# First block's mixer: HGRN gate and queries by plain float32 products, doublings among the values' products, transposes behind gate tiles

## The chip, the cores and the metric

The kernel runs on one core of one Trainium2 chip, as one launch. Its time is device microseconds (us) of that core, and a kernel's time is the median of its runs. The engines are TensorE (PE, with its weight loads as PEld), VectorE (DVE), ScalarE (ACT), GpSimd (POOL) and SyncE (SP), which issues most transfers. Each works through its own list of instructions in order; an instruction waits for those of other engines by semaphores.

## The reference, cut to what matters

The program is a two-block transformer on 256 tokens of width 1024 in float32. The change lies in the first layer's mixer alone, which is an HGRN2 half and an RWKV7 half, side by side, under one input and one output projection:

```python
u = h @ w_in                       # h [256,1024]; HGRN q, f, i, g of 512 columns each, then RWKV
hq, hf, hi, hg, ur = split(u)
f = lb + (1 - lb) * sigmoid(hf)
o_a = hgrn2_chunked(silu(hq), 1 - f, hi, log(f))      # scores decayed by cumulated log f
o_a = rms_norm(o_a) * silu(hg)
...                                                   # r, k, v, decay, a, kk, g out of ur
y = rwkv7_scan(r, decay, k, v, kk, a)                 # per head: state*w + sa*b + v*k
o_b = (head_layer_norm(y) + bonus) * g
return concat(o_a, o_b) @ w_out
```

Behind it come the first layer's feed-forward part, an attention layer and the second block with its experts. None of that is touched.

## The kernel before

**Stages.** The mixer takes about the first 186 us of the span. `proj` (its slabs of 256 columns of `w_in` are 1 MB each) makes a projection: SP loads a slab, ACT rounds half of it (128x1024) to float32r (`L116`, a cast), DVE takes the rest, what the rounding lost (`L117`), and PE adds three products for each of eight k-tiles and each tile of 128 features: high weights by high input (`L137`), low weights by high input (`L138`), high weights by low input (`L139`), all 128x256. A projection of 512 columns is four such tiles. The input `h` is split the same way once, in `hT`. `dense_tok` does the values (512 columns in two slabs, 48 products of 512 columns), with tokens on the partitions.

**Order.** RWKV's projections come first. Then come the HGRN gate `f` (`hE`, columns 512 to 1023), the queries (columns 0 to 511), the values `hv`, the decayed scores in nine levels (`l`, 0 to 8, `L828` and `L861`), the outputs `oo`, the output gate (columns 1536 to 2047, "gate tiles") and `w_out`. Beside these runs RWKV's chunked form in pieces: `pairs` (the pairwise products `L638`, whose results DVE evicts in `L631`, `L642` and `L645`, then `L650`, `L658`, `L659`), an inverse of 32x32 triangular blocks on DVE (`L582` and `L584`, 31 steps of two dependent instructions each), `levels` (the "doublings", which put inverses of 32 together to 64 and 128: `L678`, `L692`, `L702`) and `chain` (states and outputs, ending in transposes of `yy`, `L782`). These are generators: `tick(n)` lets the next one emit up to n pieces at the point of the program where it is called. A scheduler then orders each engine's list by its own estimates and by what is pinned: `keep_in_program_order` pins an instruction to its place in the program, `issue_after` puts one behind another.

**Buffers.** `psa` gives one of four `acc` buffers of PSUM, `psb` one of the `pb` buffers. Two of the `acc` hold `X` (products `L650`, copied by ACT in `L652`) until that copy. A slab's buffer is free for the next slab when its last reader is done: before, that is DVE's `L117`. SP's list is in order: a slab that waits for its buffer holds back what stands behind it, and so does the inverse's way to memory and back (`L587` out, `L593` in), which waits for the last step of the inverse.

Of the kernel before, what the change touches and what calls it, by code (L numbers as in the profile page):

```python
# [19 lines left out]
S = 256  # L20
# [32 lines left out]
def tile_body(ctx, tc, a, out, stop=None, dbg=None):  # L53
# [281 lines left out]
    def mixer0():  # L335
# [16 lines left out]
        def t2(shape, name):  # L352
            return RW.tile(shape, F32, name=name, tag="t2", bufs=5)
# [28 lines left out]
        spin(6)  # L382
        hT = pair("xT")
        for k in range(KT):
            t = t2([128, S], "hf0")
            V.scalar_tensor_tensor(t, raw[k // 2][:, k % 2 * 256:k % 2 * 256 + 256], col("attn_norm0", k), rsB, op0=mult, op1=mult)
            A.copy(hT[0][:, k, :], t)
            if k % 2:
                pooled = G.tensor_tensor(hT[1][:, k, :], t, hT[0][:, k, :], sub)  # L389
            else:  # L390
                done = V.tensor_tensor(hT[1][:, k, :], t, hT[0][:, k, :], sub)
# [22 lines left out]

        def proj(c0, use, eng=(None, None), steps=0):

            t = slab(a["w_in_ar"][:, c0:c0 + 256], KT, 256, 2 if c0 == 3584 else 1)
            for i in range(2):
                with tc.issue_after(done.ins) if c0 == 3584 and i else nullcontext():
                    w = split_tile(t[:, :, i * 128:(i + 1) * 128], KT, 128, eng[i])  # L420
                p = psa()[:, 0:256]
                mm_feat3(p, w, hT, KT)
                use(i, p)
                tick(steps)
# [196 lines left out]
        def pairs():  # L621
# [32 lines left out]
            for j2 in range(2):  # L654
# [12 lines left out]
                yield  # L667

        def levels():


            def first(l, b):
                o = 8 * b
                Wm = t2([128, 8, l], "Wm")
                p = psb()[:, 0:8 * l]
                for i in range(8):
                    for r in ((0, 64) if l == 32 else (64,)):
                        T.matmul(p[(r if l == 32 else 0):(r + 64 if l == 32 else 64), i * l:i * l + l],  # L678
                                 El[r:r + 64, o + i, (r if l == 32 else 0):(r + 64 if l == 32 else 64)],
                                 Tu[r:r + 64, o + i, (r + 32 if l == 32 else 64):r + 64], start=True, stop=True)  # L680
                n = 128 if l == 32 else 64
                A.copy(Wm[0:n], p[0:n].rearrange("p (h c) -> p h c", h=8))
                return l, b, Wm
# [38 lines left out]
        def chain():  # L722
# [55 lines left out]
            for b in range(2):  # L778
                bs = slice(b * 128, b * 128 + 128)
                p = psb()  # L780
                for j in range(4):
                    T.transpose(p[:, j * 128:(j + 1) * 128], ys[b][:, j * 128:(j + 1) * 128], ident)  # L782
                z = t2([128, 4, 128], "z")
# [9 lines left out]
        for j2 in range(2):  # L793
            proj(512 + 256 * j2, lambda i, p: V.tensor_scalar(hE[:, 2 * j2 + i, :], p, -80.0, None, op0=amax), steps=3)
        A.activation(hE, hE, AF.Exp, scale=-1.0)
# [10 lines left out]
        for j2 in range(2):  # L806
            def useq(i, p):
                th = RW.tile([128, S], F32, name="th")
                A.activation(th, p, AF.Tanh, scale=0.5)
                V.scalar_tensor_tensor(q[:, 2 * j2 + i, :], th, 1.0, p, op0=add, op1=mult)  # L810
            proj(256 * j2, useq, steps=2)
        hv = h4([128, 2, 512], "hv")
# [9 lines left out]
        for l in range(9):  # L822
# [33 lines left out]
            if m < 128:  # L856
                for b in range(2):
                    bs = slice(b * 128, b * 128 + 128)
                    p = psa()
                    for h in range(4):  # L860
                        T.matmul(p[:, h * 128:(h + 1) * 128], z[:, h, bs], z[:, h, bs], start=True, stop=True)  # L861
                    V.copy_predicated(part(ST[:, b], l - 1, 1), half4(lvl[:, l - 1, :], l - 1, 1, 4),
                                      part(p.rearrange("p (h c) -> p h c", h=4), l - 1, 1))
                tick()
            else:
# [3 lines left out]
                A.copy(STx, p.rearrange("p (h c) -> p h c", h=4))  # L869
        tick(2)  # L870

# [16 lines left out]
        for j2 in range(2):  # L888
            def useg(i, p):
# [4 lines left out]
                A.activation(hg[:, j, :], th, AF.Copy, scale=hon[:, j:j + 1])  # L894
            proj(1536 + 256 * j2, useg, steps=(2,2)[j2])

        for b in range(2):
            bs = slice(b * 128, b * 128 + 128)
            p = psa()
            for j in range(4):  # L900
# [1126 lines left out]
```

## Time and profile before

| | us |
|---|---|
| median of 3 runs | 1313.76 (1311.78 to 1317.47) |
| the profiled execution | 1317.22 |
| its span | 1315.4 |
| PE busy | 1160.4 (88%) |
| DVE busy | 716.4 (54%) |
| ACT busy | 500.0 (38%) |

The mean granted clock of PE is 0.94. The times of single instructions, below and in the prediction, are of the profiled execution, 3.46 us above the median. A PE record's own duration (0.28 us) is longer than the distance to the next one (0.113 us), as products are pipelined; what counts is the distance.

### The profile page before, as it was taken

What the parts mean: (1) busy time and instruction counts of PE and PEld (TensorE: products, weight loads), DVE (VectorE), ACT (ScalarE), POOL (GpSimd) and SP (SyncE); (2) the same over time, 40 slices, a digit from 0 to 9 for tenths busy, and PEclk for the clock granted to TensorE, in tenths of its full rate; (3) what the DMA queues carried; (4) which work ended last, traced back from release to release, by engine and by line L of the source; (5) the groups of instructions that cost most, each with busy time, mean ns of one, the idle gap of its engine ahead of it and who ended that gap; (6) DMA issues with size and microseconds to landing.
All of it is one profiled execution on the core that took longest, in us unless ns stands there. A gap on an engine that the chain in (4) does not pass through costs nothing.

```text
span 1315.4 us, 18829 instructions
## 1 busy us (share of the span) xinstructions
PE 1160.4 (88%) x7392; PEld 840.8 (64%) x7392; DVE 716.4 (54%) x1296; ACT 500.0 (38%) x874; POOL 189.7 (14%) x211
## 2 busy tenths in 40 slices
PE   8999989999999999999999999898777666667775
PEld 7898978988888878898989798662222121212212
DVE  5889777687686796667755689752111010101102
ACT  7655355454445566545444545621000000000002
POOL 1100011222120640122224124200000000000000
PEclk9999999999999999999999999999987797878877
DMA  8344046767775544676766853799999999999996
GB/s 282 86 150 113 34 138 233 281 243 257 282 272 177 173 162 157 213 250 241 261 218 225 319 181 139 274 364 423 421 422 420 420 422 418 423 419 422 419 422 246
DMA packets 129502, 362.35 MB, mean 275 GB/s; under 512 B 13440, under 2 KB 69504, under 8 KB 105856
## 3 DMA queue, kind: packets, MB, share of 16 engines
q1 hardware_dynamic: 124736, 359.65, 72.5%
q10 hardware_dynamic: 4672, 1.44, 0.5%
q8 instruction: 60, 0.98, 0.3%
q14 instruction: 34, 0.28, 0.1%
HBM read 359.49 MB, written 1.57 MB: 274 GB/s over the span
## 4 chain that ended last, share of the span: by engine, by line
PE 52%; DMA 29%; DVE 11%; ACT 3%; issue 2%; POOL 2%; SPq 0%; ACTq 0%; DVEq 0%; POOLq 0%
DMA ew<-in_exp_w_dram 15%; PE acc L138 9%; PE acc L137 9%; PE acc L139 9%; DMA ew<-in_exp_w2b_dram 8%; DMA wm<-in_mod_w_dram 5%; PE pb L137 3%; PE pb L138 3%; PE pb L139 3%; DVE s L117 3%; PE pb L1725 2%; PE pb L1699 2%; PE pb L1691 1%; PE pf L1699 1%; PE acc L1730 1%
## 5 line engine op out<-in xcount | busy, mean ns | idle before, releaser
L117 DVE TENSOR_TENSOR s<-w,s 128x1024 fp32r<-128x1024 f32 x237 | 296.9, 1258 | 98.4 <-ACT s L116 98.0
L116 ACT CAST s<-w 128x1024 fp32r<-128x1024 f32 x240 | 251.1, 1047 | 120.2 <-PE acc L139 98.7
L138 PE MATMUL pb<-xTh,s 128*128 128x256 f32 x512 | 144.2, 282 | 1.3 <-DVE s L117 1.3
L137 PE MATMUL pb<-xTh,s 128*128 128x256 f32 x512 | 144.4, 282 | 0.6 <-ACT xTh L147 0.6
L139 PE MATMUL pb<-xTl,s 128*128 128x256 f32 x512 | 144.0, 281 | 0.0
L937 POOL TENSOR_TENSOR ul<-u,uh 128x256 fp32r<-128x256 f32 x64 | 87.0, 1360 | 254.8 <-ACT uh L936 254.8
L138 PE MATMUL acc<-s,ul 128*128 128x512 f32 x256 | 100.8, 394 | 2.1 <-POOL ul L937 2.1
L137 PE MATMUL acc<-s,uh 128*128 128x512 f32 x256 | 100.3, 392 | 0.1
L139 PE MATMUL acc<-s,uh 128*128 128x512 f32 x256 | 99.8, 390 | 0.0
L137 PEld LDWEIGHTS pb<-xTh,s 128*128 128x128 f32 x512 | 96.1, 188 | 4.8 <-issue 1.7
L138 PEld LDWEIGHTS pb<-xTh,s 128*128 128x128 f32 x512 | 96.2, 188 | 4.4 <-DVE s L117 2.4
L139 PEld LDWEIGHTS pb<-xTl,s 128*128 128x128 f32 x512 | 98.0, 191 | 0.5 <-DVE xTl L148 0.4
L1725 PE MATMUL pb<-ew,big 128*32 128x512 f32 (+1 forms) x544 | 78.3, 691 | 20.7 <-DMA ew<-in_exp_w2b_dram 17.0
L137 PE MATMUL acc<-xTh,s 128*128 128x256 f32 x320 | 93.6, 294 | 2.5 <-ACT xTh L1220 1.5
L138 PE MATMUL acc<-xTh,s 128*128 128x256 f32 x320 | 91.7, 288 | 1.4 <-DVE s L117 1.4
L1704 DVE SCALAR_TENSOR_TENSOR big<-big,pb 128x512 f32<-128x512 f32 x8 | 5.5, 688 | 160.4 <-ACT big L1703 160.4
L139 PE MATMUL acc<-xTl,s 128*128 128x256 f32 x320 | 90.9, 287 | 1.3 <-POOL xTl L389 1.3
L1699 PE MATMUL pb<-ew,big 128*32 128x512 f32 x448 | 68.6, 709 | 26.4 <-DMA ew<-in_exp_w_dram 22.4
L1699 PE MATMUL pf<-ew,big 128*32 128x512 f32 x448 | 70.5, 738 | 23.8 <-DMA ew<-in_exp_w_dram 23.8
L1565 ACT ACTIVATE big<-pb,mc,gs 128x128 f32<-128x128 f32 x28 | 12.8, 458 | 194.3 <-DVE big L1567 194.3
L316 DVE SCALAR_TENSOR_TENSOR macc<-wm,cond,macc 128x512 f32<-128x512 f32 x84 | 65.8, 805 | 28.0 <-DMA wm<-in_mod_w_dram 27.9
L1728 DVE TENSOR_TENSOR big<-pb,gate 128x512 f32<-128x512 f32 (+1 forms) x17 | 11.2, 660 | 109.6 <-PE pb L1725 109.6
(601 smaller groups left out, 2171.3 us busy)
## 6 DMA issues: line engine op xcount, KB each, us to landing
ew<-in_exp_w_dram SPq DMA_DIRECT2D x128, 1024.0 KB, 19.8
w<-in_w_up_dram SPq DMA_DIRECT2D x32, 1024.0 KB, 5.7
w<-in_w_down_dram SPq DMA_DIRECT2D x32, 1024.0 KB, 6.4
ew<-in_exp_w2a_dram SPq DMA_DIRECT2D x32, 1024.0 KB, 19.8
ew<-in_exp_w2b_dram SPq DMA_DIRECT2D x28, 1024.0 KB, 20.0
wm<-in_mod_w_dram SPq DMA_DIRECT2D x24, 1024.0 KB, 7.9
w<-in_w_in_ar_dram SPq DMA_DIRECT2D x14, 1024.0 KB, 5.6
w<-in_w_qkv_dram SPq DMA_DIRECT2D x12, 1024.0 KB, 5.1
```

The lines of the kernel that those rows point to most:

```text
L116: A.copy(hi, src)
L117: (eng or V).tensor_tensor(lo, src, hi, sub)
L137: T.matmul(p, lhs[0], rhs[0], start=start, stop=False)
L138: T.matmul(p, lhs[1], rhs[0], start=False, stop=False)
L139: T.matmul(p, lhs[0], rhs[1], start=False, stop=stop)
L316: V.scalar_tensor_tensor(ac, wq, cond[:, k:k + 1], ac, op0=mult, op1=add)
L937: lows[:] = [G.tensor_tensor(ul, u, uh, sub)]
L1565: A.activation(dst, p, AF.Identity, scale=gs[:, kt:kt + 1], bias=sh[:, kt:kt + 1])
L1691: T.matmul(p[:, i * 128:(i + 1) * 128], x[:, tb, (k0 + i) * 128:(k0 + i + 1) * 128], oo[:, tb, :], start=(tb == 0), stop=(tb == 1))
L1699: T.matmul(p[32 * e:32 * e + 32, :], xg[:, k, 32 * e:32 * e + 32], t[:, e, :], start=(k == 0), stop=(k == KT - 1))
L1725: T.matmul(p[32 * e:32 * e + 32, :], ht[:, i, 32 * e:32 * e + 32], t[:, e], start=(i == 0), stop=(i == 3))
L1730: T.matmul(acc[tb][c // 512][:, c % 512:c % 512 + n], ogT[:, tb * 128:(tb + 1) * 128], y, start=first, stop=last, skip_group_check=True)
```

## The change

The normalised input is kept unsplit as well, in `hx`, instead of in a ring buffer. `proj` gets a way, `whole`, in which PE multiplies the raw slab by `hx` in plain float32: one product for each k-tile instead of three, no cast and no subtraction. The HGRN gate and the queries use it; their ticks go from (3, 2) to (3, 1). The first doubling's first product is pinned to its place, and the other first products are put behind it. Each of the two transposes of RWKV's outputs is pinned behind a gate tile, with the ticks of the score loop and of the output gate cut so that they fall there. The last transposes of HGRN's outputs take their PSUM from `psb` instead of `psa`. The new line numbers are larger by 8 to 15: the inverse is `L590` and `L592`, `eka` `L650`, `Ebr` `L639`, the first doublings `L689`, `L705` and `L715`, the outputs' transposes `L795`, the scores `L843` and `L876`, plain products `L423`.

```diff
@@ -381,8 +381,9 @@
         A.copy(rsB, p[:, 0:S])
         spin(6)
         hT = pair("xT")
+        hx = R.tile([128, KT, S], F32, name="hx")
         for k in range(KT):
-            t = t2([128, S], "hf0")
+            t = hx[:, k, :]
             V.scalar_tensor_tensor(t, raw[k // 2][:, k % 2 * 256:k % 2 * 256 + 256], col("attn_norm0", k), rsB, op0=mult, op1=mult)
             A.copy(hT[0][:, k, :], t)
             if k % 2:
@@ -412,10 +413,17 @@
                 while fills and next(fills[0], fills) is fills:
                     fills.pop(0)

-        def proj(c0, use, eng=(None, None), steps=0):
+        def proj(c0, use, eng=(None, None), steps=0, whole=False):

             t = slab(a["w_in_ar"][:, c0:c0 + 256], KT, 256, 2 if c0 == 3584 else 1)
             for i in range(2):
+                if whole:
+                    p = psa()[:, 0:256]
+                    for k in range(KT):
+                        T.matmul(p, t[:, k, i * 128:(i + 1) * 128], hx[:, k, :], start=(k == 0), stop=(k == KT - 1))
+                    use(i, p)
+                    tick(steps)
+                    continue
                 with tc.issue_after(done.ins) if c0 == 3584 and i else nullcontext():
                     w = split_tile(t[:, :, i * 128:(i + 1) * 128], KT, 128, eng[i])
                 p = psa()[:, 0:256]
@@ -666,6 +674,8 @@
                     V.scalar_tensor_tensor(bon[:, j, :], bon[:, j, :], col("ln_b", j), g, op0=add, op1=mult)
                 yield

+        begun = []
+
         def levels():


@@ -675,9 +685,12 @@
                 p = psb()[:, 0:8 * l]
                 for i in range(8):
                     for r in ((0, 64) if l == 32 else (64,)):
-                        T.matmul(p[(r if l == 32 else 0):(r + 64 if l == 32 else 64), i * l:i * l + l],
-                                 El[r:r + 64, o + i, (r if l == 32 else 0):(r + 64 if l == 32 else 64)],
-                                 Tu[r:r + 64, o + i, (r + 32 if l == 32 else 64):r + 64], start=True, stop=True)
+                        with tc.issue_after(begun[0].ins) if begun else nullcontext():
+                            e = T.matmul(p[(r if l == 32 else 0):(r + 64 if l == 32 else 64), i * l:i * l + l],
+                                         El[r:r + 64, o + i, (r if l == 32 else 0):(r + 64 if l == 32 else 64)],
+                                         Tu[r:r + 64, o + i, (r + 32 if l == 32 else 64):r + 64], start=True, stop=True)
+                        if not begun:
+                            begun.append(tc.keep_in_program_order(e))
                 n = 128 if l == 32 else 64
                 A.copy(Wm[0:n], p[0:n].rearrange("p (h c) -> p h c", h=8))
                 return l, b, Wm
@@ -779,7 +792,9 @@
                 bs = slice(b * 128, b * 128 + 128)
                 p = psb()
                 for j in range(4):
-                    T.transpose(p[:, j * 128:(j + 1) * 128], ys[b][:, j * 128:(j + 1) * 128], ident)
+                    e = T.transpose(p[:, j * 128:(j + 1) * 128], ys[b][:, j * 128:(j + 1) * 128], ident)
+                    if j == 0:
+                        tc.keep_in_program_order(e)
                 z = t2([128, 4, 128], "z")
                 V.tensor_tensor(z, p.rearrange("p (j t) -> p j t", j=4), gt[:, :, bs], mult)
                 V.tensor_tensor(z, z, bon[:, :, bs], add)
@@ -791,7 +806,7 @@
         hE = h4([128, 4, S], "hE")
         n1 = h4([128, 4, S], "n1")
         for j2 in range(2):
-            proj(512 + 256 * j2, lambda i, p: V.tensor_scalar(hE[:, 2 * j2 + i, :], p, -80.0, None, op0=amax), steps=3)
+            proj(512 + 256 * j2, lambda i, p: V.tensor_scalar(hE[:, 2 * j2 + i, :], p, -80.0, None, op0=amax), steps=3, whole=True)
         A.activation(hE, hE, AF.Exp, scale=-1.0)
         A.activation(n1, hE, AF.Ln, bias=1.0)
         for j in range(4):
@@ -808,7 +823,7 @@
                 th = RW.tile([128, S], F32, name="th")
                 A.activation(th, p, AF.Tanh, scale=0.5)
                 V.scalar_tensor_tensor(q[:, 2 * j2 + i, :], th, 1.0, p, op0=add, op1=mult)
-            proj(256 * j2, useq, steps=2)
+            proj(256 * j2, useq, steps=1, whole=True)
         hv = h4([128, 2, 512], "hv")
         dense_tok(hT, KT, a["w_in_ar"][:, 1024:1536], 512, lambda tb, h, p: A.copy(hv[:, tb, :], p), steps=lambda: tick(1))

@@ -861,13 +876,13 @@
                         T.matmul(p[:, h * 128:(h + 1) * 128], z[:, h, bs], z[:, h, bs], start=True, stop=True)
                     V.copy_predicated(part(ST[:, b], l - 1, 1), half4(lvl[:, l - 1, :], l - 1, 1, 4),
                                       part(p.rearrange("p (h c) -> p h c", h=4), l - 1, 1))
-                tick()
+                if l < 6:
+                    tick()
             else:
                 p = psa()
                 for h in range(4):
                     T.matmul(p[:, h * 128:(h + 1) * 128], z[:, h, 0:128], z[:, h, 128:256], start=True, stop=True)
                 A.copy(STx, p.rearrange("p (h c) -> p h c", h=4))
-        tick(2)

         oo = r4([128, 2, 512], "oo")
         for b in range(2):
@@ -892,11 +907,11 @@
                 A.activation(th, p, AF.Tanh, scale=0.5)
                 V.scalar_tensor_tensor(th, th, 1.0, p, op0=add, op1=mult)
                 A.activation(hg[:, j, :], th, AF.Copy, scale=hon[:, j:j + 1])
-            proj(1536 + 256 * j2, useg, steps=(2,2)[j2])
+            proj(1536 + 256 * j2, useg, steps=1)

         for b in range(2):
             bs = slice(b * 128, b * 128 + 128)
-            p = psa()
+            p = psb()
             for j in range(4):
                 T.transpose(p[:, j * 128:(j + 1) * 128], oo[:, b, j * 128:(j + 1) * 128], ident)
             z = t2([128, 4, 128], "hz")
```

On DVE, in the middle of the inverse (`inv` and `qb` are its two halves of a step; `hE` is the gate's tile, `s` a slab's split, `Ebr` the evicted pairwise products), before:

```order
L582 TENSOR_TENSOR inv<-db,qb 128x120 [waits DVE_49]
L794 TENSOR_SCALAR hE<-acc 128x256 [waits PE_49]
L584 TENSOR_TENSOR qb<-qb,inv 128x20x6 [waits DVE_49]
L582 TENSOR_TENSOR inv<-db,qb 128x133 [waits DVE_49]
L117 TENSOR_TENSOR s<-w,s 128x1024 [waits DMAHW0_49,Activation_49]
L584 TENSOR_TENSOR qb<-qb,inv 128x19x7 [waits DVE_49]
L631 TENSOR_TENSOR Ebr_875<-pb,cst 128x4x128 [waits PE_49]
L582 TENSOR_TENSOR inv<-db,qb 128x126 [waits DVE_49]
L631 TENSOR_TENSOR Ebr_875<-pb,cst 128x4x128 [waits PE_49]
L584 TENSOR_TENSOR qb<-qb,inv 128x18x7 [waits DVE_49]
```

and of the change, some steps further on, where `eka` is evicted for the products into `X`:

```order
L590 TENSOR_TENSOR inv<-db,qb 128x135 [waits DVE_49]
L809 TENSOR_SCALAR hE<-acc 128x256 [waits PE_49]
L592 TENSOR_TENSOR qb<-qb,inv 128x15x9 [waits DVE_49]
L590 TENSOR_TENSOR inv<-db,qb 128x126 [waits DVE_49]
L592 TENSOR_TENSOR qb<-qb,inv 128x14x9 [waits DVE_49]
L590 TENSOR_TENSOR inv<-db,qb 128x130 [waits DVE_49]
L592 TENSOR_TENSOR qb<-qb,inv 128x13x10 [waits DVE_49]
L590 TENSOR_TENSOR inv<-db,qb 128x120 [waits DVE_49]
L650 TENSOR_TENSOR eka<-pb,cst 128x256 [waits PE_49]
L592 TENSOR_TENSOR qb<-qb,inv 128x12x10 [waits DVE_49]
L650 TENSOR_TENSOR eka<-pb,cst 128x256 [waits PE_49]
L590 TENSOR_TENSOR inv<-db,qb 128x121 [waits DVE_49]
```

The slabs' subtractions are gone from among the steps. What is left between two steps is evictions of PE's results.

On PE, where the scores and the doublings stand (`Tu`, `El`, `Ql` and `Wm` are the operands of the doublings, `z` and `zz` those of the scores), before:

```order
L861 MATMUL acc<-z_1527 128x128 [waits DVE_49]
L861 MATMUL acc<-z_1527 128x128 x3
L678 MATMUL pb<-Tu,El 64x32 [waits DVE_49,Pool_49]
L678 MATMUL pb<-Tu,El 64x32
L861 MATMUL acc<-z_1528 128x128 [waits Activation_49]
L678 MATMUL pb<-Tu,El 64x32 [waits DVE_49]
L678 MATMUL pb<-Tu,El 64x32 x29
L861 MATMUL acc<-z_1528 128x128
L692 MATMUL pb<-Ql,Wm 32x32 [waits Activation_49]
L692 MATMUL pb<-Ql,Wm 32x32 x15
L861 MATMUL acc<-z_1528 128x128 x5
L678 MATMUL pb<-Tu,El 64x64 [waits DVE_49,PE_49]
```

and of the change (`s` and `xTh` or `xTl` are the values' products):

```order
L138 MATMUL acc<-s,xTl 128x512
L139 MATMUL acc<-s,xTh 128x512
L689 MATMUL pb<-Tu,El 64x32 [waits Pool_49]
L689 MATMUL pb<-Tu,El 64x32 x15
L137 MATMUL acc<-s,xTh 128x512
L138 MATMUL acc<-s,xTl 128x512
L139 MATMUL acc<-s,xTh 128x512
L137 MATMUL acc<-s,xTh 128x512
L138 MATMUL acc<-s,xTl 128x512
L139 MATMUL acc<-s,xTh 128x512
L689 MATMUL pb<-Tu,El 64x32 [waits PE_49]
```

The doublings have moved from among the scores to among the products for the values, six of them between two doublings.

On PE, at the two transposes of RWKV's outputs (`yy`), before:

```order
L868 MATMUL acc<-zz 128x128 [waits DVE_49,PE_49,Activation_49]
L868 MATMUL acc<-zz 128x128 x3
L782 MATMUL pb<-ident,yy_1669 128x128 [waits DVE_49,PE_49]
L782 MATMUL pb<-ident,yy_1669 128x128 x3
L879 MATMUL acc<-hv,ST 128x128 [waits PE_49,Pool_49]
...
L137 MATMUL acc<-xTh,s 128x256
L782 MATMUL pb<-ident,yy_1717 128x128 [waits DVE_49]
L782 MATMUL pb<-ident,yy_1717 128x128 x3
L138 MATMUL acc<-xTh,s 128x256
```

and of the change:

```order
L138 MATMUL acc<-xTh,s 128x256
L139 MATMUL acc<-xTl,s 128x256
L795 MATMUL pb<-ident,yy_1510 128x128 x4
L137 MATMUL acc<-xTh,s 128x256 [waits PE_49]
...
L139 MATMUL acc<-xTl,s 128x256
L795 MATMUL pb<-ident,yy_1558 128x128 x4
L137 MATMUL acc<-xTh,s 128x256 [waits DVE_49,Activation_49]
```

The transposes have moved from ahead of HGRN's outputs (`hv` by `ST`) and from the middle of the second gate tile to the ends of the first and the second gate tile.

## Rows read from the trace of the kernel before

**Rows 1.** Windows: busy time of each engine by stretch (columns in the first line)

```profile
core 0: us, PE busy (x) PEld busy (x) DVE busy (x) ACT busy (x) POOL busy (x), PEclk, DMA share, GB/s
...
80.00:90.00 10.00, 9.92 (x107) 9.40 (x105) 9.28 (x28) 2.77 (x3) 0.00 (x0) 1.00 0.61 205
90.00:100.00 10.00, 8.78 (x48) 8.23 (x48) 9.81 (x26) 6.70 (x10) 0.00 (x0) 0.66 0.00 0
...
160.00:180.00 20.00, 16.81 (x145) 16.25 (x144) 13.67 (x24) 7.74 (x13) 7.30 (x8) 1.00 0.01 2
180.00:187.00 7.00, 4.67 (x35) 4.30 (x36) 5.67 (x7) 3.93 (x8) 0.00 (x0) 1.00 0.76 260
sum 127.00, PE 118.91 PEld 111.50 DVE 103.78 ACT 59.06 POOL 8.26; mean PE 14.86 PEld 13.94 DVE 12.97 ACT 7.38 POOL 1.03
```

**Rows 2.** Timeline of PE (start, us, then the instruction): three float32r products

```profile
101.42 0.28 PE L138 MATMUL acc<-xTh,s 128*128 128x256 f32 x1
101.53 0.28 PE L139 MATMUL acc<-xTl,s 128*128 128x256 f32 x1
101.64 0.28 PE L137 MATMUL acc<-xTh,s 128*128 128x256 f32 x1
```

**Rows 3.** Timeline of PE: plain float32 products of 256 columns, and what follows

```profile
26.93 1.46 PE L455 MATMUL pb<-wa,lora 128*128 128x256 f32 x6
...
28.34 0.28 PE L138 MATMUL acc<-xTh,s 128*128 128x256 f32 x1
```

**Rows 4.** Timeline of PE where the scores begin (bracket: idle before)

```profile
123.45 2.05 PE L828 MATMUL acc<-hq,hE 128*128 128x128 f32 x16
...
128.06 2.05 PE L861 MATMUL acc<-z 128*128 128x128 f32 x16 [0.50 <-DVE ST L862]
130.59 0.39 PE L678 MATMUL pb<-Tu,El 64*64 64x32 f32 x4 [0.48 <-DVE Tu L597]
```

**Rows 5.** Groups of DVE, 73.4 to 121.8: busy us, mean ns, idle before

```profile
L117 DVE TENSOR_TENSOR s<-w,s 128x1024 fp32r<-128x1024 f32 x11 | 13.4, 1220 | 0.2
L584 DVE TENSOR_TENSOR qb<-qb,inv 128x126 f32<-128x126 f32 (+22 forms) x31 | 7.7, 248 | 0.1
L582 DVE TENSOR_TENSOR inv<-db,qb 128x126 f32<-128x126 f32 (+22 forms) x31 | 7.7, 247 | 2.5 <-DMA db<-dd 2.4
L631 DVE TENSOR_TENSOR Ebr<-pb,cst 128x512 f32<-128x512 f32 x4 | 2.7, 684 | 0.0
L642 DVE TENSOR_TENSOR eka<-pb,cst 128x256 f32<-128x256 f32 x6 | 2.5, 418 | 0.0
```

**Rows 6.** Groups of ACT in 60 to 122: the slabs' casts

```profile
L116 ACT CAST s<-w 128x1024 fp32r<-128x1024 f32 x14 | 14.6, 1048 | 12.0 <-PE acc L139 11.9
```

**Rows 7.** Waits of PE, 60 to 187: us in all, times, longest

```profile
PE pb L782 <- DVE yy L775: 2.8, 2, 1.4
PE acc L137 <- DVE th L893: 1.9, 1, 1.9
PE pb L638 <- DVE Ebr L631: 1.2, 1, 1.2
PE acc L138 <- DVE s L117: 0.8, 1, 0.8
```

**Rows 8.** Windows of 2 us, columns as in rows 1

```profile
92.00:94.00 2.00, 2.00 (x13) 1.76 (x12) 2.00 (x9) 1.97 (x5) 0.00 (x0) 0.69 0.00 0
94.00:96.00 2.00, 2.00 (x11) 2.00 (x11) 2.00 (x5) 1.97 (x3) 0.00 (x0) 0.50 0.00 0
96.00:98.00 2.00, 2.00 (x11) 2.00 (x10) 2.00 (x6) 0.76 (x1) 0.00 (x0) 0.50 0.00 0
98.00:100.00 2.00, 2.00 (x12) 1.87 (x13) 1.81 (x6) 0.03 (x1) 0.00 (x0) 0.60 0.00 0
```

**Rows 9.** Timeline of ACT: the copies that the doublings wait for

```profile
127.18 2.03 ACT L596 COPY Ql<-qs 32x512 f32<-32x512 f32 x3 [2.16 <-DMA qs<-dd]
```

**Rows 10.** Timeline of SP: the inverse is sent out

```profile
121.75 0.34 SPq L587 DMA_DIRECT2D dd<-qb  x1
```

## Prediction

> **What bounds the kernel now.** I read the busy time by stretch first, then PE's waits, then the windows of the clock, and last the timeline of PE at the places that the change moves. By stretch [rows 1] PE is busy 118.91 of the 127 us from 60 to 187, and DVE 103.78. PE is thus what the mixer runs on: its idle time is 8.1 us in all, and the list of its waits [rows 7] names 6.7 of it: 2.8 for RWKV's outputs, 1.9 at the first product of `w_out`, 1.2 for `Ebr`, 0.8 for a gate slab's split. From 80 to 100 DVE is nearly full too (9.28 and 9.81 of 10 us): there the inverse runs between evictions and the slabs' subtractions. In the same stretch the clock column falls, to a mean of 0.66 from 90 to 100 [rows 1]; window by window it reads 0.69, 0.50, 0.50, 0.60 [rows 8], the lower of the two levels, 1.2 GHz, and that right behind PE's wait for `Ebr`. Four windows of 2 us at these shares lose 2 x (0.31 + 0.50 + 0.50 + 0.40) = 3.4 us.
>
> Behind the mixer nothing is changed, and its weights are issued in order behind the mixer's on SP; I let a shift of `w_out`'s start pass to the end one for one.
>
> **Plain float32 products.** A float32r product of 256 columns starts 0.11 to 0.115 us (taken as 0.1135) after the one before it (101.42 to 101.64 is two steps [rows 2]), three for a k-tile, so 0.34 us. For plain float32 the eight products of `L828` (two blocks by four heads) show as 16 records in 2.05 us [rows 4]: two records for a product. With 256 columns six records of `L455` begin at 26.93, and the product behind them, one place ahead of 28.34, at 28.23 [rows 3]: 0.217 us a record, 0.434 a product. The change makes 64 of these (two projections, four tiles, eight k-tiles) in place of 192 of the others: 27.8 - 21.8 = +6.0 us on PE. This is the one term of which I am sure.
>
> **Splits that go.** Eight subtractions of 1.22 us on DVE [rows 5] and eight casts of 1.05 us on ACT [rows 6] go, 9.8 and 8.4 us. PE waits for a split in this stretch nearly nowhere [rows 7], so they are worth nothing by themselves. What they change is the inverse. Its 62 instructions last 15.4 us [rows 5] and, each waiting for the last, some 0.035 apart, 17.6 in a row; begun at 73.5 as before, with four tiles of `hE` (0.42 each, taken as `eka`), four `Ebr` (0.68) and nine `eka` and `Ekr` (0.42) still between [rows 5], it ends at about 99 instead of 121.6 [rows 10]. The way to memory and back and the copies by ACT took from 121.75 to 130.59 [rows 4, 9, 10], 9 us; so doublings can begin at about 108.
>
> **New waits on PE.** The evictions that PE needs for its next pairwise products now stand between inverse steps that nothing else thins out, at places where PE comes sooner. I walked both lists with the durations above, PE warm. PE does the first gate slab by 78, `Ebr`'s products by 80, the third gate tile by 83.4, further pairwise products by 86.0, and then needs the `eka` that stands behind sixteen steps of about 0.32 and one `hE`: 88.7, an idle 2.7 us. It ends the gate at 92.7 and waits 1.7 us for the second `Ebr`. The queries' tiles need `acc` buffers, two of which `X` holds; ACT's copies of `X` now stand behind its copies for the doublings, which themselves wait for the inverse's way through memory. So the third query tile waits 1.6 us, until 108.4. Sum 6.0 in place of the 1.2 for `Ebr`: +4.8. Bounds: 0, if the evictions come in between as smoothly as before, and +7, if the `Ebr` wait is as long as that for `eka`. The values' products begin at about 119 in this walk, against 112.3.
>
> **The clock.** PE idles 2.7 and 1.7 us in a stretch where 1.2 us went ahead of a fall [rows 7, 8]. I expect one fall again, but half of it costs nothing: slower products run into waits that DVE's evictions end anyway. So -1.7; bounds -3.4 (no fall) and +3.4 (two falls, none covered). The Trainium skill, "TensorE: Matmul & The Clock Gate", section "Loop structure matters more than you think", marks a copy out of PSUM by DVE as one that doesn't break PE's warmth. By that, waiting for evictions would cost no clock, the term would be -3.4 and the sum 1.7 lower. Here the trace differs: the fall to 0.50 stands directly behind a wait for such an eviction, so I go by the row.
>
> **Doublings among the values' products.** Their number is the same and so is PE's time for them. Before, they were what waited (0.48 us for `Tu`, and 0.50 for the scores' predicated copies at their side [rows 4]). Now each has six products of 512 columns before the next, time enough for ACT's copy or DVE's transposes. The operands are there at 108 to 110, ten us ahead. I take -1.0; bounds -1.0 and +2 (one late operand at each of two levels, at 1 us, since DVE's transposes and ACT's copies queue behind 1.2 and 1.05 us splits of the gate slabs [rows 5, 6]). The scores, in turn, lose the doublings as filling between dependent levels. DVE's work per level goes on beside PE's, and it is early by what the inverse gave back; I cost that at nothing, with +2 as a bound.
>
> **Transposes behind gate tiles.** The two waits for `yy` (2.8 us [rows 7]) go: a gate tile of 24 products is 2.7 us long [rows 2], more than either wait of 1.4. -2.8, bounds -2.8 and 0. The slab split that PE waited 0.8 us for [rows 7] stands well ahead of the gate now: -0.8. `w_out`'s first product waited 1.9 us for DVE's `L893`, the reader of the `acc` buffer that it takes [rows 7]. With the last transposes in `pb` it takes a buffer that was free two tiles earlier: -1.9, bounds -1.9 and 0, for DVE has the two outputs' sums, splits and the slabs' subtractions in that order and could be late itself.
>
> `hx` takes `h` out of a ring of buffers: PE waits there for other things, nothing. The slab of the second half of the values and both gate slabs now stand on SP behind the inverse's send at 99; values begin 20 us later, so that hides it. If the inverse were late by 10 us, this would cost as much as it is late.
>
> **Sum.** +6.0 + 4.8 - 1.7 - 1.0 - 2.8 - 0.8 - 1.9 = +2.6 us on the profiled execution's 1317.22 (span 1315.4 and 1.8 around it), 1319.8. The runs' median is 3.46 lower; on its scale 1313.76 + 2.6 = 1316.4. A change of under 0.5%, 6.6 us, can't be told from none here.
>
> **Rivals.**
> 1. Slower: PE's clock. Plain products are the greater part of PE's work from 62 to 117, 27.8 us, and the waits for `eka`, `Ebr` and the copies of `X` stand among them. If the clock falls behind each of two of them and nothing covers it, the term is +3.4 instead of -1.7: +7.7, 1321.5. For it: one wait of 1.2 us did it [rows 7, 8]. Against: waits of 1.4 for `yy` between 160 and 180 did not, the clock there is 1.00 [rows 1]. It decides from two uncovered falls on.
> 2. Slower: the waits at the gate don't go but move to what comes next on DVE, which from 99 on has all that it did not do earlier (the cumulated sums, the scores' operands, the splits): -5.5 falls away, +8.1, 1321.9. For it: DVE was busy 13.67 of 20 us there and 5.67 of the last 7 [rows 1]. Against: it has lost 9.8 us of work before that.
> 3. Faster: DVE was the true bound of 73 to 122, so that with 9.8 us less of it PE runs through without new waits (0 and the old 1.2 gone) and without a fall: +6.0 - 1.2 - 3.4 - 1.0 - 2.8 - 0.8 - 1.9 = -5.1, 1308.7. For it: DVE's 9.81 of 10 us [rows 1]. PE sets a limit to it: all its idle time (8.1) and the whole loss of the clock (3.4) less 6.0 is 5.5 us. More than 0.5% can't come out of this stretch but by the scatter of the runs.
> 4. Nothing but the sum of small things: the scheduler's own order hides the new waits, and gains and the 6.0 cancel: 0 to +1, 1314. It is the same verdict as mine.
>
> **How the numbers follow.** My forecast and rival 4 together 0.65, rival 1 0.14, rival 2 0.10, rival 3 0.11. The two slower ones lie at their middle just beyond 0.5%; some of my own range (its bounds add to +13 at worst) does too, and part of theirs falls below. So slower 0.23, faster 0.08, same 0.69. For the range I take the faster rival at its limit, and the slower ones with a little beyond them: 1308 to 1323.
>
> **What would show it.** In the changed profile: plain products at 0.434 us, with no cast or subtraction for four slabs; the inverse's end, by the issue behind it, near 99; waits of PE for `eka`, `Ebr` and the copies of `X` of 1.5 to 3 us each; a clock below 1 between 86 and 100; no idle time for `yy` nor ahead of `w_out`, whose first product would come at 186.1 + 2.6 = 188.7. I am wrong if the inverse still ends past 110, if PE passes 73 to 118 without waits, or if DVE is what PE waits for from the scores on.

## The result, and the profile after

The changed kernel took 1318.24 us in the median of 10 runs, the kernel before 1311.88 in 10: a ratio of 1.0053, 95% interval 1.0038 to 1.0068, some 6 to 7 us slower. The prediction had 1316.4 and "no change" as the likeliest, a range of 1308 to 1323, and 0.23 for slower by over 0.5%. The time lies within the range, on the edge of what was called slower. The change from the kernel before was forecast at 2.6 us and is 6.4 by the medians. The profiled execution took 1318.1 us, with a span of 1316.2.

By stretch, in the columns of [rows 1]:

```profile
80.00:90.00 10.00, 8.75 (x58) 7.56 (x58) 9.49 (x34) 0.00 (x0) 0.00 (x0) 1.00 0.28 94
90.00:100.00 10.00, 8.99 (x62) 7.34 (x61) 8.70 (x27) 7.68 (x10) 0.00 (x0) 0.85 0.45 135
...
160.00:180.00 20.00, 15.71 (x122) 15.55 (x121) 10.58 (x21) 4.90 (x8) 6.25 (x8) 0.83 0.14 47
```

From 160 to 180 PE is busy 15.71 us against 16.81, and the clock column, 1.00 before, is 0.83. From 90 to 100 it is 0.85 against 0.66. PE's waits from 60 to 195, which answer to [rows 7]:

```profile
PE acc L884 <- DVE zz L870: 4.3, 1, 4.3
PE acc L658 <- DVE eka L650: 1.4, 2, 1.3
PE pb L646 <- DVE Ebr L639: 0.8, 2, 0.6
PE acc L137 <- ACT s L116: 0.3, 1, 0.3
```

Of the four waits of [rows 7] three are gone: nothing for `yy`, nothing ahead of `w_out`, nothing for the gate slab's split. The one for `Ebr` is 0.8 instead of 1.2, and the two waits of [rows 4] are gone too. What came instead is 1.4 us for `eka` and one wait of 4.3 us, for `zz`. `w_out`'s first product on PE's timeline:

```profile
189.62 0.47 PE L137 MATMUL acc<-s,aR 128*128 128x512 f32 x1
```

It is 3.5 us later than the 186.1 that the prediction starts from. How much of that is scatter between two executions is looked at with b2 below.

The wait for `zz` is seen best on DVE's timeline (start, us, instruction, and in brackets the idle time before it and whom it waited for):

```profile
163.16 0.69 DVE L788 TENSOR_TENSOR yy<-yy,st 128x512 f32<-128x512 f32 x1 [1.85 <-POOL st L157]
...
164.77 0.68 DVE L869 TENSOR_TENSOR zz<-zz,hE 128x512 f32<-128x512 f32 x1
...
169.56 0.69 DVE L788 TENSOR_TENSOR yy<-yy,st 128x512 f32<-128x512 f32 x1 [1.72 <-POOL st L157]
170.17 0.68 DVE L870 TENSOR_TENSOR zz<-zz,hq 128x512 f32<-128x512 f32 x1
```

on POOL's:

```profile
167.89 1.64 POOL L157 TENSOR_TENSOR st<-st,mhalf 128x8 f32<-128x8 f32 x1
```

and on PE's:

```profile
163.75 2.96 PE L876 MATMUL acc<-z 128*128 128x128 f32 x25
171.00 2.05 PE L884 MATMUL acc<-zz 128*128 128x128 f32 x8 [4.29 <-DVE zz L870]
```

`L870` makes the last operand of the scores, and PE's `L884` needs it. On DVE it stands behind `L788`, the product of `yy` by a reciprocal root that POOL computes in 1.64 us. DVE sits idle for POOL, 1.85 us for the first block of `yy` and 1.72 us for the second, with the operand ready to be made behind it. In the kernel before, the last product into `zz` (`L855`) stood ahead of both (`L775`, of which this is the first):

```profile
158.17 0.69 DVE L855 TENSOR_TENSOR zz<-zz,hq 128x512 f32<-128x512 f32 x1
165.06 0.69 DVE L775 TENSOR_TENSOR yy<-yy,st 128x512 f32<-128x512 f32 x1 [1.66 <-POOL st L157]
```

In the changed kernel PE ran dry at about 166.7 and waited until 171.00. The granted clock by windows of 2 us, columns as in [rows 1], in the two places where it falls:

```profile
96.00:98.00 2.00, 2.00 (x12) 1.86 (x12) 1.48 (x6) 2.00 (x5) 0.00 (x0) 0.76 0.38 146
98.00:100.00 2.00, 2.00 (x6) 1.55 (x5) 2.00 (x3) 1.98 (x3) 0.00 (x0) 0.50 0.28 52
100.00:102.00 2.00, 2.00 (x11) 1.45 (x9) 1.29 (x3) 1.96 (x3) 0.00 (x0) 0.89 1.10 101
...
168.00:170.00 2.00, 0.00 (x0) 0.00 (x0) 0.44 (x1) 0.00 (x0) 1.53 (x1) 0.68 0.00 0
170.00:172.00 2.00, 1.00 (x5) 1.03 (x6) 0.85 (x2) 0.00 (x0) 0.00 (x0) 0.50 0.00 0
172.00:174.00 2.00, 2.00 (x11) 2.00 (x11) 0.00 (x0) 0.92 (x2) 0.00 (x0) 0.50 0.03 8
174.00:176.00 2.00, 2.00 (x13) 2.00 (x13) 1.35 (x2) 1.21 (x2) 0.00 (x0) 0.62 0.00 0
```

The second fall begins within PE's idle time and lasts into the outputs' products, which run at the lower level to about 175. The first one stands behind PE's waits for `eka` and `Ebr` and loses 2 x (0.24 + 0.50 + 0.11) = 1.7 us.

Plain products, as [rows 3]:

```profile
107.20 3.67 PE L423 MATMUL acc<-hx,w 128*128 128x256 f32 x16
110.71 0.59 PE L666 MATMUL pb<-rx,rk 128*128 128x256 f32 x2
```

Sixteen records in 3.51 us are 0.219 each, 0.439 a product; the prediction had 0.434. The inverse is sent out, and so has ended, here:

```profile
96.65 0.34 SPq L595 DMA_DIRECT2D dd<-qb  x1
```

### The profile page after: what moved, and what is told of

Same layout as the page of the kernel before. It is cut to its first block, busy times and chain, and to the rows that moved or that the text cites. A ratio compares the mean times of both kernels' runs of the same rounds, so it can differ in the third digit from the quotient of the medians.

```text
span 1316.2 us, 18672 instructions
## 1 busy us (share of the span) xinstructions
PE 1157.8 (88%) x7328; PEld 840.5 (64%) x7328; DVE 710.7 (54%) x1288; ACT 492.8 (37%) x866; POOL 191.6 (15%) x211
## 4 chain that ended last, share of the span: by engine, by line
PE 53%; DMA 30%; DVE 9%; ACT 3%; issue 2%; POOL 1%; SPq 0%; ACTq 0%; DVEq 0%; POOLq 0%
DMA ew<-in_exp_w_dram 17%; DMA ew<-in_exp_w2b_dram 10%; PE acc L137 9%; PE acc L138 9%; PE acc L139 9%; PE pb L137 4%; PE pb L139 4%; PE pb L138 4%; DMA wm<-in_mod_w_dram 3%; PE acc L423 1%; PE pb L1740 1%; DVE s L117 1%; PE pb L1714 1%; PE pf L1714 1%; PE pb L1706 1%
## 5 line engine op out<-in xcount | busy, mean ns | idle before, releaser
L117 DVE TENSOR_TENSOR s<-w,s 128x1024 fp32r<-128x1024 f32 x229 | 285.6, 1251 | 102.2 <-ACT s L116 102.0
L116 ACT CAST s<-w 128x1024 fp32r<-128x1024 f32 x232 | 242.7, 1047 | 101.0 <-PE acc L139 82.8
L952 POOL TENSOR_TENSOR ul<-u,uh 128x256 fp32r<-128x256 f32 x64 | 90.6, 1415 | 247.5 <-ACT uh L951 247.5
L1740 PE MATMUL pb<-ew,big 128*32 128x512 f32 (+1 forms) x544 | 74.6, 659 | 20.4 <-DMA ew<-in_exp_w2b_dram 17.0
L137 PE MATMUL acc<-xTh,s 128*128 128x256 f32 x256 | 74.2, 292 | 2.5 <-ACT xTh L1235 1.5
L139 PE MATMUL acc<-xTl,s 128*128 128x256 f32 x256 | 72.4, 287 | 1.4 <-POOL xTl L390 1.3
L138 PE MATMUL acc<-xTh,s 128*128 128x256 f32 x256 | 72.8, 286 | 0.6 <-DVE s L117 0.6
```

The costliest lines, as they stand in the source:

```text
L116: A.copy(hi, src)
L117: (eng or V).tensor_tensor(lo, src, hi, sub)
L137: T.matmul(p, lhs[0], rhs[0], start=start, stop=False)
L138: T.matmul(p, lhs[1], rhs[0], start=False, stop=False)
L139: T.matmul(p, lhs[0], rhs[1], start=False, stop=stop)
L952: lows[:] = [G.tensor_tensor(ul, u, uh, sub)]
```

## The experiments

Theory A: the loss is the wait for `zz` and the fall of the clock behind it. Theory B: it is the 6.0 us that plain products add on PE, and the wait only fills time that is lost anyway. The two do not exclude each other: both costs can be there.

Times below are ratios to the kernel before, run beside it on the same chip, with 95% intervals. Since executions scatter by several us, the time at which `w_out`'s first product starts is given beside them. That start is not yet the mixer's own length: the first transpose of `vx`, which is the same work in all kernels, already begins between 60.0 and 61.2 us, and `w_out` itself can be longer or shorter. So here are three stretches of every trace, in us (b2 and e1 to e9 are described below): from that transpose to `w_out`'s first product, from it to the first transpose of `x` behind `w_out` (the mixer's end), and from there to the attention layer's first product (the feed-forward stage, which no kernel here changes).

| | to `w_out` | to the mixer's end | feed-forward |
|---|---|---|---|
| before | 125.0 | 142.1 | 226.7 |
| b2, before again | 122.8 | 141.5 | 226.8 |
| the changed kernel | 128.4 | 145.5 | 224.2 |
| e1 | 123.3 | 140.4 | 226.0 |
| e1b, e1 again | 124.7 | 141.7 | 225.7 |
| e7 | 126.4 | 143.5 | 220.8 |
| e3 | 135.5 | 152.6 | 225.9 |
| e2 | 118.0 | 137.2 | 225.6 |
| e8 | 116.1 | 136.8 | 223.6 |
| e5 | 121.5 | 138.6 | 225.0 |
| e4 | 123.3 | 140.3 | 221.2 |
| e4b, e4 again | 124.7 | 141.7 | 221.2 |
| e9 | 120.9 | 137.9 | 223.8 |

**b2: the kernel before, a second trace.**

> The kernel before once more, for a second trace. w_out's first product at 186 within 0.5 us; if the stretch from 265 to 385 us (feed-forward part with the modulation weights) takes 2.5 us more than in the changed kernel's trace again, it is the order that absorbs the shift, if not, it is the scatter of transfers.

1313.37 us in its one run. The granted clock from 86 to 104, in the first trace and in this one:

```profile
86.00:104.00 18.00, 16.78 (x128) 15.92 (x127) 15.88 (x47) 10.17 (x14) 0.00 (x0) 0.81 0.15 57
86.00:104.00 18.00, 16.78 (x144) 15.44 (x144) 17.37 (x50) 11.04 (x14) 0.00 (x0) 1.00 0.15 56
```

PE's wait there, and `w_out`'s first product:

```profile
PE pb L638 <- DVE Ebr L631: 1.2, 1, 1.2
```

```profile
183.13 0.50 PE L137 MATMUL acc<-s,aR 128*128 128x512 f32 x1 [1.90 <-DVE th L893]
```

The same wait of 1.2 us is there, but the clock does not fall, and `w_out` begins at 183.13 instead of 186.09, not within the 0.5 us that was expected. Of these 3.0 us, 0.8 stand ahead of `vx`. So the fall that the prediction took as a part of the kernel before, 3.4 us by its windows, is not in every execution of it; e5 below, whose instructions are the same up there, has half of it, 0.91. In `w_out` it is the other way round: behind the wait of 1.9 us, which both traces have, the clock falls in this one and is 1.00 in the first:

```profile
185.00:190.00 5.00, 5.00 (x18) 3.99 (x17) 2.83 (x4) 2.05 (x3) 0.00 (x0) 0.73 0.96 333
```

Against the two traces of before the changed kernel's mixer is 3.4 and 5.6 us longer to `w_out`, and 3.4 and 4.0 to its end. Its feed-forward stage is some 2.5 us shorter than in either, so part of the loss is not seen at the attention layer. The medians of the runs differ by 6.4. What the traces place in the mixer is thus less than the runs' loss, and the rest is not placed.

**e1: the products of `yy` behind the last score operand.** In the changed kernel:

```diff
-                V.tensor_tensor(y3, y3, st[:, :, 3:4].to_broadcast([128, 8, 64]), mult)
-                ys.append(y)
+                ys.append((y, y3, st))
                 yield
+            for y, y3, st in ys:
+                with tc.issue_after(zlast[0].ins):
+                    V.tensor_tensor(y3, y3, st[:, :, 3:4].to_broadcast([128, 8, 64]), mult)
+            yield
...
```

Not shown are the lines that keep the last `L870` in `zlast`, and one more `tick()` behind the scores, at which these products are emitted.

> The changed kernel, with RWKV's two products of yy by the reciprocal root (which wait for POOL) held on DVE behind the last score operand zz. Theory A (the loss is the 4.3 us wait of PE for zz and the half clock behind it, some 2.2 us): 6.5 us faster than the changed kernel, 1311 to 1313, level with the kernel before; no PE wait over 1 us from 137 to the gate, w_out's first product near 183 to 184. Theory B (the loss is the 6.0 us that plain products add on PE, and the wait only fills time that is lost anyway): at most 2 us faster than the changed kernel, 1316 to 1318, with the wait turned up again at the gate.

1.0010 (0.9996 to 1.0024); as e1b, run again beside e4b, 1.0006 (0.9989 to 1.0023). PE's wait for `zz`, DVE's order there, and `w_out`:

```profile
PE acc L889 <- DVE zz L875: 1.3, 1, 1.3
```

```profile
166.08 0.69 DVE L875 TENSOR_TENSOR zz<-zz,hq 128x512 f32<-128x512 f32 x1
166.69 0.69 DVE L794 TENSOR_TENSOR yy<-yy,st 128x512 f32<-128x512 f32 x1
```

```profile
183.43 0.47 PE L137 MATMUL acc<-s,aR 128*128 128x512 f32 x1
```

Now `L875` (the former `L870`) comes first and the products of `yy` follow with POOL's results nearly there. The wait is 1.3 us instead of 4.3, the clock from 165 to 180 is 1.00 instead of 0.77, and of the loss of 0.53% some 0.10% is left. That is theory A, if with a little more left than it named: theory B allowed at most 2 us. What stays of the wait is DVE's own work ahead of the operand. What the products cost by themselves e1 doesn't tell, since it keeps them.

**e7: the wait filled with products.** In the changed kernel, behind the seventh level's scores:

```diff
-                        T.matmul(p[:, h * 128:(h + 1) * 128], z[:, h, bs], z[:, h, bs], start=True, stop=True)
+                        sc = T.matmul(p[:, h * 128:(h + 1) * 128], z[:, h, bs], z[:, h, bs], start=True, stop=True)
+                    if l == 7 and b:
+                        pw = psb()
+                        with tc.issue_after(sc.ins):
+                            for h in range(18):
+                                T.matmul(pw[:, h % 4 * 128:(h % 4 + 1) * 128], z[:, h % 4, bs], z[:, h % 4, bs], start=True, stop=True)
```

> The changed kernel with 18 further products of the seventh score level into a scratch buffer (4 us, results unused) right behind that level's own, where PE waits for zz. Theory A: the idle time stays lost, but the clock does not fall behind it: 1.00 from 168 to 178 and 1.5 to 2.5 us faster than the changed kernel, ratio 1.003 to 1.004. If the fall is not PE's idle time here, or costs nothing: as the changed kernel, ratio 1.005.

1.0032 (1.0020 to 1.0044). The stretch from 165 to 180 in the changed kernel and here, and `w_out`:

```profile
165.00:180.00 15.00, 10.71 (x77) 10.55 (x76) 7.43 (x13) 3.61 (x6) 4.27 (x6) 0.77 0.18 63
165.00:180.00 15.00, 14.73 (x131) 14.57 (x129) 8.90 (x15) 4.58 (x7) 4.27 (x6) 1.00 0.22 71
```

```profile
186.45 0.48 PE L137 MATMUL acc<-s,aR 128*128 128x512 f32 x1
```

The clock stays at the upper level, and `w_out` begins 3.2 us earlier than in the changed kernel. Of these, 1.1 stand ahead of `vx` already, and `zz` comes earlier by the same 1.1; the other 2.0 are the clock's. By the runs it is 2.8 us (1.0053 to 1.0032), with intervals that overlap. So the wait cost twice: as idle time, and by the clock that fell behind it.

**e3: plain products alone, in the kernel before.**

```diff
...
-            t = t2([128, S], "hf0")
+            t = hx[:, k, :]
...
-            proj(512 + 256 * j2, lambda i, p: ..., steps=3)
+            proj(512 + 256 * j2, lambda i, p: ..., steps=3, whole=True)
...
-            proj(256 * j2, useq, steps=2)
+            proj(256 * j2, useq, steps=2, whole=True)
```

> The kernel before with plain float32 products for gate and queries alone (and the unsplit input kept). DVE's order now has zz behind both products of yy, and PE's transposes of yy stand ahead of the last scores. Theory A: the wait for zz or yy is there at full length, 4 to 6 us with a fall of the clock, 1317 to 1322. Theory B: +6.0 for the products less what DVE's relief gives back, 1315 to 1318, and waits near the scores' end of under 3 us.

1.0080 (1.0061 to 1.0099), 10.6 us by the medians and more than either theory named; `w_out` begins at 195.76. PE's waits:

```profile
PE acc L658 <- DVE eka L650: 3.8, 3, 2.0
PE pb L790 <- DVE yy L783: 3.6, 1, 3.6
PE acc L876 <- DVE zz L863: 1.9, 1, 1.9
PE acc L137 <- DVE th L901: 1.9, 1, 1.9
```

Every kind of wait is here at once: for `eka` behind uninterrupted steps of the inverse, for `yy` ahead of the last scores (3.6 us in one), for `zz`, and ahead of `w_out`. DVE's relief of 9.8 us does not show in any of them. By the medians of two sets of runs, the other parts of the change take back some 4 of these 10.6 us.

**e2: everything but the plain products.** The changed kernel with `whole=True` struck at both places.

> The changed kernel with HGRN's gate and queries split into float32r products again; the doublings fall back among the scores by the scheduler's order, so what is left is the transposes behind gate tiles and in pb. Both theories: the waits of 2.8 us for yy and 1.9 us ahead of w_out are gone, no 6.0 us, 4 to 5 us faster than before, 1307 to 1308. If instead the waits only moved (rival 2 of the prediction): within 1 us of before, 1311 to 1313.

0.9970 (0.9953 to 0.9988), 1309.39 us in the median: faster than both kernels. `w_out` begins at 178.73, 4.4 us before b2's (4.8 from `vx` on). The doublings fall back among the scores here, so that is what the transposes and the buffer are worth, with the ticks that place them. Two of the waits left on PE:

```profile
PE pb L646 <- DVE Ebr L639: 1.2, 1, 1.2
PE acc L894 <- DVE ST L877: 1.1, 1, 1.1
```

**e8: e2 with the cure of e1.** As e1, but the products of `yy` are put behind the scores' last predicated copy (`zl = V.copy_predicated(...)`).

> As e2, with RWKV's two products of yy behind the last predicated copy of the scores: the same cure as in e1, in the kernel without plain products. PE's wait of 1.1 us for that copy at the outputs goes, w_out's first product at 177.5 to 178 with the clock whole: 1 us faster than e2, ratio 0.996. If DVE's later work takes it back: as e2, 0.997.

```profile
176.35 0.48 PE L137 MATMUL acc<-s,aR 128*128 128x512 f32 x1
```

The wait of 1.1 us for the copy is gone, and `w_out` begins earliest of all, 2.4 us before e2's. By the runs it can't be told from e2: 0.9972 (0.9955 to 0.9989), 1308.62 us. The table says why: at the mixer's end it is only 0.4 us ahead. `w_out` waits for its own operands, as in e2, and here the clock falls behind that:

```profile
180.00:185.00 5.00, 5.00 (x17) 3.98 (x16) 3.48 (x6) 3.51 (x7) 0.00 (x0) 0.68 0.79 257
```

**e5: the last transposes in `pb` alone, in the kernel before.**

```diff
-            p = psa()
+            p = psb()
             for j in range(4):
                 T.transpose(p[:, j * 128:(j + 1) * 128], oo[:, b, j * 128:(j + 1) * 128], ident)
```

> The kernel before with the last transposes of HGRN's outputs in pb instead of acc, nothing else. If the buffer was the wait: the 1.9 us ahead of w_out's first product go, 1.5 to 2 us faster than before (ratio 0.9985 to 0.9989). If only the wait's name changes (DVE's sums and splits are late themselves): under 0.5 us.

0.9991 (0.9979 to 1.0004). The wait ahead of `w_out` is gone:

```profile
182.69 0.47 PE L137 MATMUL acc<-s,aR 128*128 128x512 f32 x1
```

With a fall of the clock in this trace (0.91 over 86 to 104) it still begins 0.4 us before b2's:

```profile
86.00:104.00 18.00, 16.78 (x138) 15.92 (x138) 17.26 (x50) 11.03 (x14) 0.00 (x0) 0.91 0.17 57
```

The buffer was the wait; the runs give 1.2 us, with an interval that reaches to nothing.

**e4 and e9: only one half in plain products, with e1's cure.** `whole=True` is kept for the gate alone (e4) or the queries alone (e9).

> As e1 (products of yy behind zz), but with only the gate in plain float32 and the queries split again: 32 plain products for 96. Theory A': what is left of the loss once the wait for zz is gone is the plain products on PE, 3.1 us for each half: midway between e1 and e2, 1311 to 1312.5. Theory B': it is the new waits for eka and Ebr and the fall of the clock behind them (1.0 and 1.7 us), which come with the gate: then as e1, 1314 to 1315.

> The counterpart of e4: products of yy behind zz, the queries in plain float32 and the gate split. If plain products cost the same wherever they stand on PE's path (3.0 us each half), as e4, ratio 0.997 to 0.9985. If the queries' half carries the whole difference between e1 and e4 (5 to 6 us by the runs), as e1, ratio 1.000 to 1.002. If both halves together make it (two halves that each are hidden, but not both), ratio below 0.998.

e4 took 0.9966 (0.9943 to 0.9990), e9 0.9985 (0.9967 to 1.0003), at the upper edge of its first case. Neither theory on e4 is right: its runs are as fast as e2's, while its `w_out` begins at 183.73, as late as e1's. e9's begins at 182.09. From `vx` to `w_out` the queries' half alone thus takes 4.8 us more than e8, which has no plain products, the gate's half alone 7.2, and both halves (e1) 7.3. The halves don't add up, and each costs more than the 3.1 us of its products; waits for `eka`, `Tu` and `zz` come with them. As e4's runs and its mixer said different things, e4 and e1 were run once more, beside each other.

> e4 once more beside e1, for a second trace of each: in the first, w_out's first product stood at 183.7 us, as in e1's (183.4), while its runs were 6 us faster. If the mixer makes the difference, w_out's first product is at 177 to 180 this time (the half clock of 165 to 180 gone). If it is the feed-forward stage, it is at 182 to 184 again, and the stage from 260 to 372 us is 4 us or more shorter than in e1b.

> e1 once more beside e4: ratio 1.001 as before, within 0.0015, on the same chip as e4b; w_out's first product at 183 to 184; the fall of the clock at 94 to 100 us there again (0.91 over 86 to 104), since PE waits for eka and Ebr in all of its runs.

e4b took 0.9967 (0.9953 to 0.9981). `w_out` began at 185.48 in it and at 184.89 in e1b:

```profile
185.48 0.47 PE L137 MATMUL acc<-s,aR 128*128 128x512 f32 x1
```

It is the feed-forward stage, then: by the same instructions of both traces, e4b is 0.6 us behind e1b at 200 us and 3.9 ahead of it at 424. The waits of DVE for the modulation weights from 200 to 380 us, of e1b:

```profile
DVE macc L316 <- DMA wm<-in_mod_w_dram: 28.6, 12, 3.3
```

and of e4b:

```profile
DVE macc L316 <- DMA wm<-in_mod_w_dram: 15.3, 13, 2.9
```

These transfers of 1 MB come later or sooner, and what DVE does with them stands ahead of what PE waits for. e4's two traces have 18.5 and 15.3 us here, e1's 27.9 and 28.6, the kernel before 26.6 in both. The transfers themselves take as long, 8.1 us from issue to landing in the median of e1b and 7.9 in e4b; it is their starts that drift apart. Counted from the first transpose of `x`, the first three are issued at the same times in both, the fourth 1.4 us later in e1b. Why two kernels with the same instructions in that stage differ so is open. It means that e4's gain by the runs is not the mixer's, and that the other ratios hold a few us of this stage too: in the table it is between 220.8 and 226.8 us long.

## Why the prediction was right or wrong

- **Plain products, +6.0 us.** Right in the price: 0.439 us each, 64 x (0.439 - 0.341) = 6.3. (The product behind the six records of [rows 3] is listed at 28.03 and not at the 28.23 that the prediction worked out; the changed kernel's 0.219 a record bears out its 0.217.) What they add on PE's path is shown only roughly. e1 and e8, with the same kind of cure, differ by 7.3 us from `vx` to `w_out`, but by 3.6 to the mixer's end, and the halves of e4 and e9 don't add up. The two kernels differ in the place of the doublings too, so 6.3 is what fits the products and not proof.
- **New waits on PE, +4.8.** Too large. The waits for `eka` and `Ebr` are there, at the places named, but with 1.4 and 0.8 us instead of 2.7 and 1.7; the queries' tiles did not wait for the copies of `X` at all. +1.0 in place of +4.8. The walk on paper erred by 1 to 2 us at each step, as much as the waits that it was to find.
- **The clock, -1.7.** The loss in the changed kernel's first fall, 1.7 us, is as forecast. What was wrong was to count 3.4 as lost in the kernel before: b2 has the wait and no fall, e5 the wait and half of it. Against b2 the term is +1.7, against e5 about nothing. One trace could not settle it. The page of the Trainium skill that was weighed here ("TensorE: Matmul & The Clock Gate", section "Loop structure matters more than you think") says that a copy by DVE out of PSUM does not break the warmth, but of a loop in which the next products follow at once. Here PE waited for the copy, so the prediction read more out of the page than it says. Where PE does not wait the trace agrees with the page: from 140 to 165 in the changed kernel PE is busy for all 25 us, DVE reads results out of PSUM beside it, and the clock is 1.00.
- **Doublings, -1.0, and transposes with the buffers, -2.8, -0.8 and -1.9.** Right, all these waits are gone from PE's list, and e2 shows 4.4 us at `w_out` (4.8 from `vx` on) for the transposes and the buffer together, where 4.7 were counted.
- **"The scores, in turn, lose the doublings as filling ... I cost that at nothing, with +2 as a bound."** This is the step that failed. It is 4.3 us of idle time and a fall of the clock behind it. e1 takes back 5.6 us by the runs (1.0053 to 1.0010 is 0.43%) and 5.1 from `vx` to `w_out` (3.7 in e1b, whose wait for `eka` is 1.0 longer): 3.0 of the 4.3 us of idle time, and 2.1 for the clock, which e7 alone puts at 2.0. I had looked at how much work DVE has, and it had enough time; what counted was the order, in which an instruction that waits for POOL stands ahead of one that PE waits for. I did not walk DVE's list past the values' products.
- **The signs.** The inverse is sent out at 96.65 (forecast near 99), PE's waits for `eka` and `Ebr` between 73 and 118 are there, the one for the copies of `X` is not, and there is no wait at the output gate; `w_out` begins at 189.62 (forecast 188.7). But the last of the signs of being wrong came true: from the scores on, DVE is what PE waits for, 4.3 us for `zz`.
- **A shift of `w_out`'s start passes to the end one for one.** Not borne out: against b2 the changed kernel is 6.5 us later at `w_out`, 2.2 at the attention layer's first product and 4.6 at the end of the span.
- **"Its bounds add to +13 at worst".** By the terms as they stand the upper bounds add to +19.6, so the range left out more of the slow side than it says.

That the time fell into the range is in part luck. The forecast of 1316.4 is 1.8 us off because the kernel before, at 1313.76 in 3 runs, came to 1311.88 in 10; the change itself was forecast some 4 us short, by errors of both signs: 3.8 too much for waits that did not come, up to 3.4 of clock counted to the kernel before, and 5.6 that were not seen. Listed against b2, +6.3 for products, +1.0 for waits, +1.7 for the first fall, -6.5 for the waits that went and +5.6 for `zz` make +8.1; measured from `vx` to `w_out` are 5.6. The remaining 2.5 us I can't place.

Of the rivals, the second came nearest: DVE as what PE waits for, with +8.1 for the whole change where 6.4 were measured. But it put the wait at the gate, whose waits went, and down to the amount of work, where it was the order.

## What to carry to other kernels

When work is taken from between dependent steps, look at what stands next to whom in each engine's list afterwards: an instruction that waits for a slow third engine holds up whatever is queued behind it, however idle the engine looks. The price of the wait was its idle time, 4.3 us, and, since TensorE's clock fell behind it, about half as much again; moving the instruction gave most of it back, filling the wait gave back the clock's part. And replacing three products by one is no gain if the one shows as two records each twice as long: here 0.44 us against 0.34. Last, a start time read from one trace holds the scatter of all that stands ahead of it: take differences within a trace, and look whether what was gained is still there at the end of the stage.

## What the runs showed of the hardware

- The same wait on PE came once with a fall of the clock and once without: 1.2 us for `Ebr` with 0.81 over 86 to 104 in the first trace of before and 1.00 in b2, 1.9 us for `th` with 1.00 and 0.73 over 185 to 190. From `vx` to `w_out` these two executions of one kernel differ by 2.2 us.
- POOL's reciprocal root of 128x8 elements took 1.64 us, more than two passes of DVE over 128x512.
- DVE waited 15 to 29 us within one stage for the modulation weights, by kernel and execution, though the transfers took 7.8 to 8.6 us in the median of each trace; the stage's length differed by up to 6 us.
